# Gate and up of a SwiGLU layer with standing weights and streaming tokens

## Chip, core and metric

The kernel runs on one core of one Trainium2 chip. The metric is the device time of one execution in microseconds (us), smaller is better. A difference of about 0.2% is the least that a measurement of this kernel can tell.

## What is computed

Two layers of a small transformer trunk over 256 tokens of width 1024, all in float32. Each layer has a mixer (a sparse attention whose keys are chosen by an indexer, beside a differential attention) and a SwiGLU feed-forward part of inner width 2816. Cut to what matters here:

```python
for layer in range(DEPTH):                       # 2
    h = rms_norm(x, g_mix[layer])
    ...                                          # projections, two attentions
    x = x + mixed @ w_out[layer]
    h2 = rms_norm(x, g_ffn[layer])
    gate = h2 @ w_gate[layer]                    # 256 x 1024 by 1024 x 2816
    up = h2 @ w_up[layer]
    x = x + (silu(gate) * up) @ w_down[layer]    # 256 x 2816 by 2816 x 1024
return rms_norm(x, g_final)
```

## The kernel before

Tokens lie in two blocks of 128 (`NB = 2`, index b). Every large product is made in a split form: a float32 operand becomes a high part, rounded to the float32r type in which TensorE takes a column a cycle, and a low part, the rest. `mm3` (L205) makes three matmuls of each product: high by high, high by low weight, low by high weight. Activations stand in the array as 128x128 blocks and weights stream, 512 columns at a time.

Weights come in chunks of one megabyte. `load` (L163) issues the DMA on SP's queue into one of three `wraw` buffers; `split_sub` (L181) makes the high part on ScalarE (L186) and the low part on VectorE (L187), in pieces of 1024 columns, into six buffers `whi` and six `wlo`. `ensure` (L197) keeps loads three chunks and splits one chunk ahead in the order of the text.

The order of TensorE's instructions is written by `Weave` (L50): threads yield a delay and events, and `spend` moves a clock on by what each matmul is reckoned to take. ScalarE's and VectorE's instructions are put in order by the scheduler of the framework; each engine runs its queue in order.

The feed-forward part of a layer: `norm` (L360) transposes the residual x of one token block and half, scales it by the gain and splits it, giving `hi_ffn` and `lo_ffn`; the reciprocal of the root mean square, `rstd`, is one number a token and is applied later. Then, for six groups of 512 columns (the last has 256 of gate and 256 of up side by side), `group` (L633) makes gate for both token blocks in two PSUM banks and then up. `after_gate` (L708) applies rstd and silu on ScalarE. `after_up` (L620) multiplies on VectorE, waits DUP = 2.5 us of the Weave's clock, transposes the product in blocks of 128 on TensorE (`pth`), and splits it into `hi_ff` and `lo_ff` for down. Down (L734) lets those stand and streams `w_down`, 22 contraction tiles for two token blocks and two halves; the last six tiles (`TAIL`) are done piece by piece, so that the residual addition (L756) and the final norm (`final`, L762) of one piece run beside the next. In the last layer, the last half of block 1 is cut into two pieces of 256 columns which share one PSUM bank.

PSUM has eight banks (L117), all under one tag.

Of the kernel before, what the change touches and what calls it, by code (L numbers as in the profile page):

```python
# [8 lines left out]
F32 = mybir.dt.float32  # L9
# [8 lines left out]
P = 128  # L18
# [15 lines left out]
DG = 2.0  # L34
DUP = 2.5
DQB = 2.5
# [72 lines left out]
@with_exitstack  # L109
def tile_hybrid_trunk(ctx, tc, x, xT, w_idx, w_in, w_out, w_gate, w_up, w_down, g_final, rope, out):  # L110
    nc = tc.nc
# [11 lines left out]
    NSUB = 1024  # L123
    LASTN = DFF % 512
    chunks = []
# [6 lines left out]
    for L in range(DEPTH):  # L132
        for nm in GROUPS:
            for a, e in ((0, 4), (4, 8)):
                c = add_chunk(w_idx[L, a // 4] if nm == "idx" else w_in[L], range(a, e), COL[nm], NCOL[nm])
                for k in range(a, e):
                    plan[L, nm, k] = c
        for a in (4, 6, 0, 2):
            c = add_chunk(w_out[L], range(a, a + 2), 0, D)
            for k in (a, a + 1):  # L140
                plan[L, "out", k] = c
        for j in range(6):
            if DFF - j * 512 >= 512:
                for nm, w in (("gate", w_gate), ("up", w_up)):
                    for a in range(0, KT, 4):
                        c = add_chunk(w[L], range(a, a + 4), j * 512, 512)
                        for k in range(a, a + 4):
                            plan[L, nm, j, k] = c
            else:

                for a in range(0, KT, 4):
                    c = add_chunk((w_gate[L], w_up[L]), range(a, a + 4), j * 512, 2 * LASTN)
                    for k in range(a, a + 4):
                        plan[L, "both", j, k] = c
# [8 lines left out]
    def load(c):  # L163
        src, kts, c0, n = chunks[c]
        t = pool.tile([P, len(kts), n], F32, tag="wraw", bufs=3, name=f"wraw{c}")
        if n == NCOL["idx"]:
            for k in range(0, len(kts), 2):
                nc.sync.dma_start(t[:, k:k + 2], src[:, k:k + 2])
        elif isinstance(src, tuple):
            for i, w in enumerate(src):  # L170
                nc.sync.dma_start(t[:, :, i * LASTN:(i + 1) * LASTN], w[kts[0] * P:(kts[-1] + 1) * P, c0:c0 + LASTN]
                                  .rearrange("(k p) n -> p k n", p=P))
# [31 lines left out]

    def mm3(outs, act, kt, first, last, second=False):  # L205


        hi, lo = act[kt]
        for ps, whi, wlo in outs:
            nc.tensor.matmul(ps, hi, whi, start=first, stop=False, skip_group_check=second)  # L210
        for ps, whi, wlo in outs:
            nc.tensor.matmul(ps, hi, wlo, start=False, stop=False, skip_group_check=second)  # L212
        for ps, whi, wlo in outs:
            nc.tensor.matmul(ps, lo, whi, start=False, stop=last, skip_group_check=second)  # L214
            W.spend(3 * max(0.107, 0.216 * ps.shape[-1] / 512))
# [87 lines left out]

    def hilo(sc, hi, lo, k0, k1):
        nc.vector.tensor_copy(hi[:, k0:k1], sc[:, k0:k1])
        nc.vector.tensor_tensor(lo[:, k0:k1], sc[:, k0:k1], hi[:, k0:k1].bitcast(F32), op=ALU.subtract)

    def split_psum(pt, name, scales=None, tag="act", bufs=12):

        n = pt.shape[1]  # L310
        tags = tag if isinstance(tag, tuple) else (tag, tag)
        bufs = bufs if isinstance(bufs, list) else [bufs, bufs]
        hi = pool.tile([P, 4, P], F32R, tag=tags[0], bufs=bufs[0], name=f"hi_{name}")
        lo = pool.tile([P, 4, P], F32R, tag=tags[1], bufs=bufs[1], name=f"lo_{name}")
        if scales is None:
# [6 lines left out]
        else:  # L322
            sc = pool.tile([P, 4, P], F32, tag="hff", bufs=3, name=f"sc_{name}")
            for k in range(0, n, 2):
                scaled(sc, pt, scales, k, k + 2)
                hilo(sc, hi, lo, k, k + 2)
        return [(hi[:, k], lo[:, k]) for k in range(n)]

# [13 lines left out]
    acts = {}  # L342
    rstd = {}

    pts = {}
# [7 lines left out]
    def norm_split(kind, L, b, h):  # L353
        key = (kind, L, b)
        acts.setdefault(key, []).extend(
            split_psum(pts.pop(key + (h,)), f"{kind}{L}{b}{h}",
                       scales=[gcol(kind, L, 4 * h + k) for k in range(4)]))
        W.done(("act",) + key + (h,), 2.0)

    def norm(kind, L, b, h):  # L360
# [4 lines left out]
        if h == 1:  # L365
            rstd[kind, L, b] = norm_rstd(b, f"{kind}{L}{b}")


# [250 lines left out]

    def after_up(L, j, b, n, s, ps):  # L620
        hh = pool.tile([P, 512], F32, tag="hff", bufs=3, name=f"hff{L}{j}{b}")
        nc.vector.scalar_tensor_tensor(hh[:, :n], ps[:, :n], rstd["ffn", L, b], s[:, :n], op0=ALU.mult, op1=ALU.mult)
        yield DUP, ()
        pt = bank(f"pth{L}{j}{b}").rearrange("p (k t) -> p k t", k=4)
        for k in range(n // P):
            transpose(pt[:, k], hh[:, k * P:(k + 1) * P])
        t = split_psum(pt[:, :n // P], f"ff{L}{j}{b}", tag=FT[j], bufs=[FTB.get(t, 2) for t in FT[j]])
        for i, e in enumerate(t):
            ffT[L, b, 4 * j + i] = e
        W.done(("ff", L, j, b), 1.8)  # L630

# [36 lines left out]
    def main():  # L668
        for L in range(DEPTH):
# [25 lines left out]
            for b in range(NB):  # L695
                for h in range(2):
# [6 lines left out]
                    W.spawn(norm("ffn", L, b, h))  # L703
            for j in range(6):
                n = min(512, DFF - j * 512)
                silus = {}

                def after_gate(b, ps):  # L708
                    s = pool.tile([P, 512], F32, tag="silu", bufs=2, name=f"silu{L}{j}{b}")
                    nc.scalar.activation(s[:, :n], ps[:, :n], AF.Silu, scale=rstd["ffn", L, b])  # L710
                    silus[b] = s

                if n == 512:
                    yield from group("ffn", L, (L, "gate", j), n, j == 0, after_gate)
                    yield from group("ffn", L, (L, "up", j), n, False,
                                     lambda b, ps: W.spawn(after_up(L, j, b, n, silus[b], ps)))
                else:
                    def after_both(b, ps):
                        after_gate(b, ps)
                        W.spawn(after_up(L, j, b, n, silus[b], ps[:, n:]))  # L720

                    yield from group("ffn", L, (L, "both", j), 2 * n, False, after_both)
            nk = DFF // P
            halves = [(0, 512), (512, 1024)]

            cuts = [list(halves) for b in range(NB)]
            if L + 1 == DEPTH:
                cuts[NB - 1] = [(0, 512), (512, 768), (768, 1024)]
            pd = [[bank(f"dn{L}{b}{h}") for h in range(2)] for b in range(NB)]

            def piece(b, a, e):
                return pd[b][a // 512][:, a % 512:a % 512 + e - a]

            def down(b, cols, kt):  # L734
                w = parts[plan[L, "down", kt], kt]
                mm3([(piece(b, a, e), w[0][:, a:e], w[1][:, a:e]) for a, e in cols], ffT, (L, b, kt),
                    kt == 0, kt == nk - 1, cols[0][0] % 512 > 0)

            TAIL = 6
            for kt in range(nk - TAIL):  # L740
                ensure(plan[L, "down", kt], 3, 2)
                for b in range(NB):
                    yield 0, (("ff", L, kt // 4, b),)
                    down(b, halves, kt)
            ensure(plan[L, "down", nk - 1], 3, 1)
# [3 lines left out]
            for b in range(NB):  # L749
                if L + 1 == DEPTH:  # L750
                    fin = final(b, cuts[b], gfin)
                for h, (a, e) in enumerate(cuts[b]):
                    for kt in range(nk - TAIL, nk):
                        yield 0, (("ff", L, kt // 4, b),)
                        down(b, [(a, e)], kt)
                    nc.vector.tensor_tensor(X[b][:, a:e], piece(b, a, e), X[b][:, a:e], op=ALU.add)  # L756
                    if L + 1 == DEPTH:
                        next(fin)
# [38 lines left out]
    def startup(after):  # L797
        n = NCOL["idx"]
        with tc.manual_schedule(engines={ENG.Activation, ENG.DVE}):
# [18 lines left out]
            def halved(h, b):  # L818
                hi, lo = (pool.tile([P, 4, P], F32R, tag="act", bufs=12, name=f"{w}_mix0{b}{h}") for w in ("hi", "lo"))
                v = sc[h][:, :, b * P:(b + 1) * P]  # L820
# [81 lines left out]
```

## Time and profile before

| | |
|---|---|
| time, median of 3 runs | 638.94 us (638.86 to 638.96) |
| profiled execution, its own time | 638.96 us |
| its span, first to last instruction | 637.1 us |
| TensorE (PE) busy, matmuls | 626.2 us, 98%, 3091 |
| VectorE (DVE) busy | 435.5 us, 68% |
| ScalarE (ACT) busy | 361.2 us, 57% |
| moved from HBM | 108.02 MB |

The span is what the instructions take; some 1.9 us lie around it. Matmuls are pipelined: a 512-column matmul is shown with 0.39 us, but the next starts 0.227 us after it, so a stage is read from starts and not from durations. PEld rows are the loads of the block that stands for the next matmul.

### The profile page before, as it was taken

To read this page: it belongs to the slowest core of one execution; us is meant where nothing else is said; L and a number is where in the kernel's file an instruction comes from. 1 tells how busy PE (TensorE), PEld (TensorE's weight loads), DVE (VectorE), ACT (ScalarE), POOL (GpSimd) and SP (SyncE) were. 2 spreads that over 40 slices of the span, in tenths; PEclk is the share of its full clock that TensorE was granted. 3 is DMA by queue.
4 is the path that set the end of the run, shared out by engine and by line. 5 is a ranking of instruction groups with operands and counts; after the bars stand their busy time and mean duration, and the time that the engine had idled before them with its cause. 6 is when DMAs were issued, how large, how long until landed. Compare 5 with 4: busy or idle time off the path is not lost.

```text
span 637.1 us, 8397 instructions
## 1 busy us (share of the span) xinstructions
PE 626.2 (98%) x3091; PEld 512.0 (80%) x3091; DVE 435.5 (68%) x925; ACT 361.2 (57%) x620; POOL 2.0 (0%) x12
## 2 busy tenths in 40 slices
PE   9999999999999999999999999999999999999995
PEld 5888777888888888888898787878888888888884
DVE  5999997696555456544598999876756555464445
ACT  4877587684454444433477777876744454453331
POOL 1000000000000000000000000000000000000000
PEclk9999999999999999999999999999999999999999
DMA  9854443346665556654286533323755555646511
GB/s 334 288 196 151 139 172 134 133 133 198 199 197 163 192 175 199 198 195 145 67 268 205 188 133 132 133 70 129 246 178 174 196 198 179 196 158 200 193 34 66
DMA packets 49369, 109.61 MB, mean 172 GB/s; under 512 B 1968, under 2 KB 6576, under 8 KB 49328
## 3 DMA queue, kind: packets, MB, share of 16 engines
q1 hardware_dynamic: 48320, 106.96, 50.4%
q10 hardware_dynamic: 1008, 2.12, 0.9%
q8 instruction: 24, 0.39, 0.3%
q14 instruction: 17, 0.14, 0.1%
HBM read 108.02 MB, written 1.05 MB: 171 GB/s over the span
## 4 chain that ended last, share of the span: by engine, by line
PE 81%; DVE 14%; issue 2%; DMA 2%; ACT 1%; ACTq 0%
PE dn L210 6%; PE dn L214 6%; PE dn L212 6%; PE ps_gate L210 6%; PE ps_gate L214 6%; PE ps_gate L212 6%; PE ps_up L214 6%; PE ps_up L212 6%; PE ps_up L210 6%; DVE wlo L187 4%; PE wo L210 2%; PE wo L214 2%; PE wo L212 2%; DVE topk L474 2%; PE pth L218 2%
## 5 line engine op out<-in xcount | busy, mean ns | idle before, releaser
L187 DVE TENSOR_TENSOR wlo<-wraw,whi 128x1024 fp32r<-128x1024 f32 (+1 forms) x200 | 241.3, 1213 | 138.3 <-ACT whi L186 134.3
L186 ACT CAST whi<-wraw 128x1024 fp32r<-128x1024 f32 (+1 forms) x200 | 207.1, 1044 | 147.4 <-PE dn L214 47.5
L210 PE MATMUL ps_gate<-whi,hi_ffn 128*128 128x512 f32 x160 | 64.3, 402 | 0.0
L214 PE MATMUL ps_gate<-whi,lo_ffn 128*128 128x512 f32 x160 | 62.5, 391 | 0.0
L214 PE MATMUL ps_up<-whi,lo_ffn 128*128 128x512 f32 x160 | 62.3, 389 | 0.0
L212 PE MATMUL ps_gate<-wlo,hi_ffn 128*128 128x512 f32 x160 | 62.3, 389 | 0.0
L210 PE MATMUL ps_up<-whi,hi_ffn 128*128 128x512 f32 x160 | 62.2, 389 | 0.0
L212 PE MATMUL ps_up<-wlo,hi_ffn 128*128 128x512 f32 x160 | 62.2, 389 | 0.0
L210 PE MATMUL dn<-whi,hi_ff 128*128 128x512 f32 (+1 forms) x182 | 59.9, 386 | 0.5 <-DVE x L756 0.5
L214 PE MATMUL dn<-whi,lo_ff 128*128 128x512 f32 (+1 forms) x182 | 59.2, 382 | 0.0
L212 PE MATMUL dn<-wlo,hi_ff 128*128 128x512 f32 (+1 forms) x182 | 59.2, 382 | 0.0
L214 PEld LDWEIGHTS dn<-whi,lo_ff 128*128 128x128 f32 x182 | 34.2, 188 | 6.7
L210 PEld LDWEIGHTS dn<-whi,hi_ff 128*128 128x128 f32 x182 | 33.9, 188 | 7.0 <-DVE x L756 0.7
L212 PEld LDWEIGHTS dn<-wlo,hi_ff 128*128 128x128 f32 x182 | 34.2, 188 | 6.6
L214 PEld LDWEIGHTS ps_gate<-whi,lo_ffn 128*128 128x128 f32 x160 | 30.0, 188 | 6.6
L210 PEld LDWEIGHTS ps_up<-whi,hi_ffn 128*128 128x128 f32 x160 | 30.0, 188 | 6.2
L214 PEld LDWEIGHTS ps_up<-whi,lo_ffn 128*128 128x128 f32 x160 | 30.0, 188 | 6.2
L212 PEld LDWEIGHTS ps_up<-wlo,hi_ffn 128*128 128x128 f32 x160 | 30.0, 188 | 6.2
L212 PEld LDWEIGHTS ps_gate<-wlo,hi_ffn 128*128 128x128 f32 x160 | 30.1, 188 | 5.7
L210 PEld LDWEIGHTS ps_gate<-whi,hi_ffn 128*128 128x128 f32 x160 | 30.1, 188 | 5.6
L316 ACT CAST hi_ff<-pth 128x512 fp32r<-128x512 f32 (+1 forms) x24 | 13.1, 548 | 21.1 <-PE pth L218 21.1
L317 DVE TENSOR_TENSOR lo_ff<-pth,hi_ff 128x512 fp32r<-128x512 f32 (+1 forms) x24 | 15.5, 646 | 8.8 <-ACT hi_ff L316 8.8
(346 smaller groups left out, 1081.5 us busy)
## 6 DMA issues: line engine op xcount, KB each, us to landing
wraw<-in_w_in_dram SPq DMA_DIRECT2D x24, 1024.0 KB, 5.1
wraw<-in_w_down_dram SPq DMA_DIRECT2D x22, 1024.0 KB, 5.0
wraw<-in_w_gate_dram SPq DMA_DIRECT2D x20, 1024.0 KB, 5.1
wraw<-in_w_up_dram SPq DMA_DIRECT2D x20, 1024.0 KB, 5.1
wraw<-in_w_out_dram SPq DMA_DIRECT2D x8, 1024.0 KB, 5.0
wraw<-in_w_idx_dram SPq DMA_DIRECT2D x8, 296.0 KB, 3.5
wraw<-in_w_gate_dram SPq DMA_DIRECT2D x4, 512.0 KB, 4.0
wraw<-in_w_up_dram SPq DMA_DIRECT2D x4, 512.0 KB, 5.0
```

Of the source, the lines that this page charges most:

```text
L186: nc.scalar.copy(hi, raw[c][:, s:s + step])
L187: nc.vector.tensor_tensor(lo, raw[c][:, s:s + step], hi.bitcast(F32), op=ALU.subtract)
L210: nc.tensor.matmul(ps, hi, whi, start=first, stop=False, skip_group_check=second)
L212: nc.tensor.matmul(ps, hi, wlo, start=False, stop=False, skip_group_check=second)
L214: nc.tensor.matmul(ps, lo, whi, start=False, stop=last, skip_group_check=second)
L218: nc.tensor.transpose(o, i, ident)
L316: nc.scalar.copy(hi[:, :n], pt)
L317: nc.vector.tensor_tensor(lo[:, :n], pt, hi[:, :n].bitcast(F32), op=ALU.subtract)
L474: nc.vector.match_replace(out=nxt[:, :nk], in_to_replace=m8, in_values=cur[:, :nk], imm_value=TAKEN)
```

## The change

Gate and up are made transposed. A 128x128 block of w_gate or w_up stands, and the tokens stream: the high weights against high and low tokens of both blocks side by side (512 columns), the low weights against the high tokens (256 columns). `ff_mm` makes one unit, a block of 128 inner columns of one matrix, in one PSUM bank; its two halves are added at evacuation (`halves_sum`). The inner dimension then lies on the partitions, as down needs it, and the transposition of the product goes away. rstd now varies along the free dimension: for gate, `norm` transposes rstd, broadcast to 128 columns, into a row of both token blocks (`rows`, DRB = 6.0 us behind the norm); for up, the factor is applied when down's result is added to the residual (`add`). The first two column blocks (BYB = 2) are made one token block at a time. w_gate and w_up are stored on the host as one array `w_ff`, one contiguous megabyte to a block of 128 inner columns. The two last quarter pieces of down get PSUM banks of their own, and what was summed up to then for that half is added to x first.

```diff
+        for i in range(NF):
+
+            plan[L, "ff", i] = add_chunk(w_ff[L, i], range(2), 0, KT * P)
...
+        elif len(src.shape) == 4:
+            nc.sync.dma_start(t, src.rearrange("p m k n -> p m (k n)"))
...
     def norm(kind, L, b, h):
...
         if h == 1:
             rstd[kind, L, b] = norm_rstd(b, f"{kind}{L}{b}")
+            if kind == "ffn":
+                yield DRB, ()
+
+                if b == 0:
+                    rows["ffn", L] = pool.tile([P, S], F32, tag="amask", bufs=2, name=f"rrow{L}")
+                pt = bank(f"ptr{L}{b}")
+                transpose(pt[:, :P], rstd[kind, L, b].to_broadcast([P, P]))
+                nc.scalar.copy(rows["ffn", L][:, b * P:(b + 1) * P], pt[:, :P])
+                if b == NB - 1:
+                    W.done(("rrow", L))
...
-    def after_up(L, j, b, n, s, ps):
-        hh = pool.tile([P, 512], F32, tag="hff", bufs=3, name=f"hff{L}{j}{b}")
-        nc.vector.scalar_tensor_tensor(hh[:, :n], ps[:, :n], rstd["ffn", L, b], s[:, :n], op0=ALU.mult, op1=ALU.mult)
-        yield DUP, ()
-        pt = bank(f"pth{L}{j}{b}").rearrange("p (k t) -> p k t", k=4)
-        for k in range(n // P):
-            transpose(pt[:, k], hh[:, k * P:(k + 1) * P])
-        t = split_psum(pt[:, :n // P], f"ff{L}{j}{b}", tag=FT[j], bufs=[FTB.get(t, 2) for t in FT[j]])
...
+    def ff_mm(L, i, m, ps, bs):
+
+
+        c = plan[L, "ff", i]
+        whi, wlo = parts[c, m]
+        sl = slice(bs[0] * P, (bs[-1] + 1) * P)
+        ps = ps.rearrange("p (t q) -> p t q", t=2)
+        for k in range(KT):
+            yield 0, tuple(("act", "ffn", L, b, k // 4) for b in bs)
+            a = acts["ffn", L, k // 4][k % 4 // 2][:, k % 2]
+            w = slice(k * P, (k + 1) * P)
+            both = lambda: nc.tensor.matmul(ps[:, :, sl], whi[:, w], a[:, :, sl], start=(k == 0), stop=(k == KT - 1))
+            if k == 0:
+                both()
+            nc.tensor.matmul(ps[:, 0, sl], wlo[:, w], a[:, 0, sl], start=False, stop=False)
+            if k > 0:
+                both()
+            W.spend((0.32 + 0.027) if len(bs) == 2 else 0.187)
+
+    def halves_sum(ps, name):
+        t = pool.tile([P, 512], F32, tag="hff", bufs=3, name=name)[:, :S]
+        nc.scalar.copy(t, ps[:, S:])
+        nc.vector.tensor_tensor(t, ps[:, :S], t, op=ALU.add)
+        return t
+
+    silus = {}
+
+    def after_gate(L, i, ps):
+        g = halves_sum(ps, f"gt{L}{i}")
+        nc.vector.tensor_tensor(g, g, rows["ffn", L], op=ALU.mult)
+        s = silus[L, i] = pool.tile([P, 512], F32, tag="silu", bufs=2, name=f"silu{L}{i}")[:, :S]
+        nc.scalar.activation(s, g, AF.Silu)
+
+    def after_up(L, i, ps):
+
+        u = halves_sum(ps, f"up{L}{i}")
+        nc.vector.tensor_tensor(u, u, silus[L, i], op=ALU.mult)
...
+        hi, lo = (t[:, i % 2] for t in fft)
+        nc.scalar.copy(hi, u)
+        nc.vector.tensor_tensor(lo, u, hi.bitcast(F32), op=ALU.subtract)
...
+    def after_ff(L, i, m, ps):
+        yield 0, (("rrow", L),)
+        (after_gate, after_up)[m](L, i, ps)
+
+    def feed_forward(L):
+        units = [(i, m) for i in range(BYB) for m in range(2)]
+        banks = {}
+        for b in range(NB):
+            for i, m in units:
+                ensure(plan[L, "ff", i])
+                if b == 0:
+                    banks[i, m] = bank(f"ff{L}_{i}{m}")
+                yield from ff_mm(L, i, m, banks[i, m], (b,))
+                if b == NB - 1:
+                    W.spawn(after_ff(L, i, m, banks[i, m]))
+        for i in range(BYB, NF):
+            for m in range(2):
+                ensure(plan[L, "ff", i])
+                ps = bank(f"ff{L}_{i}{m}")
+                yield from ff_mm(L, i, m, ps, (0, 1))
+                W.spawn(after_ff(L, i, m, ps))
...
+            def add(b, a, e, ps):
+                nc.vector.scalar_tensor_tensor(X[b][:, a:e], ps[:, :e - a], rstd["ffn", L, b], X[b][:, a:e],
+                                               op0=ALU.mult, op1=ALU.add)
...
+                    if ends and b == NB - 1 and kt == nk - TAIL - 1:
+                        for h in (1, 0):
+                            down(b, halves[h:h + 1], kt, pd[b][h:h + 1], False, h == 1)
+                        add(b, 512, D, pd[b][1])
...
+                if ends and b == NB - 1:
+                    pieces[1:] = [(ae, bank(f"dne{ae[0]}"), True) for ae in ((512, 768), (768, 1024))]
```

## Rows read from the trace of the kernel before

**Rows 1.** The page: busy time by engine; granted clock by 40 slices.
```profile
PE 626.2 (98%) x3091; PEld 512.0 (80%) x3091; DVE 435.5 (68%) x925; ACT 361.2 (57%) x620; POOL 2.0 (0%) x12
...
PEclk9999999999999999999999999999999999999999
```

**Rows 2.** Waits of TensorE: line waited for; us in total, times, longest.
```profile
PE ppt_b L218 <- DVE p_b L530: 2.0, 2, 1.0
...
PE dn L210 <- DVE x L756: 0.5, 1, 0.5
```

**Rows 3.** Timeline, TensorE, both ends of gate and up: start, duration, operation.
```profile
132.94 0.40 PE L212 MATMUL ps_gate<-wlo,hi_ffn 128*128 128x512 f32 x1
...
258.36 0.62 PE L212 MATMUL dn<-wlo,hi_ff 128*128 128x512 f32 x2
```

**Rows 4.** Timeline, TensorE, the last matmuls of down: 512 columns, then 256.
```profile
612.74 0.39 PE L210 MATMUL dn<-whi,hi_ff 128*128 128x512 f32 x1
...
624.75 0.39 PE L214 MATMUL dn<-whi,lo_ff 128*128 128x512 f32 x1
624.98 0.28 PE L210 MATMUL dn<-whi,hi_ff 128*128 128x256 f32 x1
625.09 0.28 PE L212 MATMUL dn<-wlo,hi_ff 128*128 128x256 f32 x1
...
627.01 0.28 PE L214 MATMUL dn<-whi,lo_ff 128*128 128x256 f32 x1
```

**Rows 5.** Timeline, TensorE, eight 128-column matmuls between 512-column ones.
```profile
397.66 0.39 PE L214 MATMUL ps_va<-whi,lo_mix 128*128 128x512 f32 x1
397.89 1.05 PE L445 MATMUL ob<-vb,pT_b 128*128 128x128 f32 x8
...
399.01 0.40 PE L212 MATMUL ps_va<-wlo,hi_mix 128*128 128x512 f32 x1
```

**Rows 6.** Timeline, loads and matmuls of TensorE after the pause in the tail.
```profile
627.80 0.19 PEld L210 LDWEIGHTS dn<-whi,hi_ff 128*128 128x128 f32 x1 [0.72 <-DVE x L756]
...
627.91 0.19 PEld L212 LDWEIGHTS dn<-wlo,hi_ff 128*128 128x128 f32 x1
628.03 0.28 PE L212 MATMUL dn<-wlo,hi_ff 128*128 128x256 f32 x1
```

**Rows 7.** Timeline: last transpositions of the feed-forward norm, last step of its rstd.
```profile
135.49 0.60 PE L218 MATMUL pt_ffn<-ident,x 128*128 128x128 f32 x4
...
141.01 0.16 DVE L296 SCALAR_TENSOR_TENSOR rs_ffn01y<-rs_ffn01t,rs_ffn01y 128x1 f32<-128x1 f32 x1
```

**Rows 8.** Timeline of the tail: VectorE's last additions, TensorE's last matmul.
```profile
628.46 0.69 DVE L773 TENSOR_TENSOR fo<-x,gfin 128x512 f32<-128x512 f32 x1
...
629.94 0.28 PE L214 MATMUL dn<-whi,lo_ff 128*128 128x256 f32 x1
...
630.74 0.41 DVE L756 TENSOR_TENSOR x<-dn,x 128x256 f32<-128x256 f32 x1
```

**Rows 9.** Groups by line and shape, 132 to 258 us: count, busy us, mean ns.
```profile
L187 DVE TENSOR_TENSOR wlo<-wraw,whi 128x1024 fp32r<-128x1024 f32 x47 | 57.4, 1224 | 44.2 <-ACT whi L186 42.3
...
L306 DVE TENSOR_TENSOR lo_ffn<-sc_ffn,hi_ffn 128x256 fp32r<-128x256 f32 x4 | 1.5, 415 | 0.0
...
L186 ACT CAST whi<-wraw 128x1024 fp32r<-128x1024 f32 x46 | 48.3, 1053 | 40.8 <-PE ps_up L214 20.5 <-issue 10.0 <-PE ps_gate L214 8.3
...
L710 ACT ACTIVATE silu<-ps_both,rs_ffn00y 128x256 f32<-128x256 f32 x1 | 0.5, 475 | 1.7 <-PE ps_both L214 1.7
```

**Rows 10.** Windows: busy us of each engine (instructions), clock, DMA share, GB/s.
```profile
0.00:100.00 100.00, 97.48 (x486) 76.44 (x487) 89.26 (x257) 71.38 (x151) 1.96 (x12) 1.00 0.62 214
```

**Rows 11.** Waits of ScalarE: line waited for; us in total, times, longest.
```profile
ACT whi L186 <- PE ps_up L214: 41.0, 32, 3.0
```

**Rows 12.** Timeline, TensorE, 512-column matmuls that follow a run of 296 columns.
```profile
326.43 0.40 PE L210 MATMUL ps_qb<-whi,hi_mix 128*128 128x512 f32 x1
...
327.82 0.39 PE L210 MATMUL ps_qb<-whi,hi_mix 128*128 128x512 f32 x1
```

More of the change, by code (lines that the diff above doesn't have):

```diff
@@ L34 @@
 DG = 2.0
-DUP = 2.5
+BYB = 2
+DRB = 6.0
 DQB = 2.5
@@ L123, in tile_hybrid_trunk @@
     NSUB = 1024
-    LASTN = DFF % 512
+    NF = DFF // P
     chunks = []
@@ L325, in split_psum @@
                 scaled(sc, pt, scales, k, k + 2)
-                hilo(sc, hi, lo, k, k + 2)
-        return [(hi[:, k], lo[:, k]) for k in range(n)]
+                if into is None:
+                    hilo(sc, hi, lo, k, k + 2)
+                else:
+                    hilo(sc, *into[k // 2], k, k + 2, 0)
+        return [] if into is not None else [(hi[:, k], lo[:, k]) for k in range(n)]
     def square_sum(src, acc, name):
@@ L343, in tile_hybrid_trunk @@
     rstd = {}
+    rows = {}
     pts = {}
@@ L354, in norm_split @@
         key = (kind, L, b)
-        acts.setdefault(key, []).extend(
-            split_psum(pts.pop(key + (h,)), f"{kind}{L}{b}{h}",
-                       scales=[gcol(kind, L, 4 * h + k) for k in range(4)]))
+        into = None
+        if kind == "ffn":
+            if b == 0:
+                acts["ffn", L, h] = [pool.tile([P, 2, 2, S], F32R, tag="act", bufs=6, name=f"actT{L}{h}{i}")
+                                     for i in range(2)]
+            into = [[t[:, :, i, b * P:(b + 1) * P] for i in range(2)] for t in acts["ffn", L, h]]
+        r = split_psum(pts.pop(key + (h,)), f"{kind}{L}{b}{h}",
+                       scales=[gcol(kind, L, 4 * h + k) for k in range(4)], into=into)
+        if kind != "ffn":
+            acts.setdefault(key, []).extend(r)
         W.done(("act",) + key + (h,), 2.0)
@@ L703, in main, with down @@
                     W.spawn(norm("ffn", L, b, h))
[L704 to L722, printed above, removed]
+            yield from feed_forward(L)
             nk = DFF // P
             halves = [(0, 512), (512, 1024)]
-            cuts = [list(halves) for b in range(NB)]
-            if L + 1 == DEPTH:
-                cuts[NB - 1] = [(0, 512), (512, 768), (768, 1024)]
             pd = [[bank(f"dn{L}{b}{h}") for h in range(2)] for b in range(NB)]
-            def piece(b, a, e):
-                return pd[b][a // 512][:, a % 512:a % 512 + e - a]
-            def down(b, cols, kt):
+            TAIL = 6
+            def down(b, cols, kt, banks, first, last):
                 w = parts[plan[L, "down", kt], kt]
-                mm3([(piece(b, a, e), w[0][:, a:e], w[1][:, a:e]) for a, e in cols], ffT, (L, b, kt),
-                    kt == 0, kt == nk - 1, cols[0][0] % 512 > 0)
-            TAIL = 6
+                mm3([(ps[:, :e - a], w[0][:, a:e], w[1][:, a:e]) for (a, e), ps in zip(cols, banks)], ffT, (L, b, kt),
+                    first, last)
+            def add(b, a, e, ps):
+                nc.vector.scalar_tensor_tensor(X[b][:, a:e], ps[:, :e - a], rstd["ffn", L, b], X[b][:, a:e],
+                                               op0=ALU.mult, op1=ALU.add)
+            ends = L + 1 == DEPTH
             for kt in range(nk - TAIL):
@@ L749, in main @@
             for b in range(NB):
-                if L + 1 == DEPTH:
-                    fin = final(b, cuts[b], gfin)
-                for h, (a, e) in enumerate(cuts[b]):
+                pieces = [(ae, ps, False) for ae, ps in zip(halves, pd[b])]
+                if ends and b == NB - 1:
+                    pieces[1:] = [(ae, bank(f"dne{ae[0]}"), True) for ae in ((512, 768), (768, 1024))]
+                if ends:
+                    fin = final(b, [p[0] for p in pieces], gfin)
+                for h, ((a, e), ps, own) in enumerate(pieces):
                     for kt in range(nk - TAIL, nk):
[L754 to L757, printed above, removed]
+                        yield 0, (("ff", L, kt),)
+                        down(b, [(a, e)], kt, [ps], own and kt == nk - TAIL, kt == nk - 1)
+                    add(b, a, e, ps)
+                    if ends:
                         next(fin)
```

67 lines of the change are left out of this document (31 added, 36 removed).

## The prediction

> **What bounds the kernel now.** I began with the page: TensorE is busy for 98% of the span at a granted clock of ten tenths in all slices, VectorE for 68% [rows 1]. Then the list of what TensorE waited for: no line waited more than 2.0 us in all, and the only entry of the feed-forward part is 0.5 us before the last piece of the last down projection [rows 2]. None lies in gate and up. So in the feed-forward part the time is the number of matmuls times their pitch (start to start), plus the transpositions between them; other engines count only if they come to stall TensorE. I therefore read the stage boundaries and the pitches of the shapes that the change uses.
>
> Gate and up of layer 0, from their second matmul at 132.94 to the third matmul of down at 258.36, take 125.42 us [rows 3]; layer 1 does the same work and I count it alike. Per layer there are 2 x 5 x 8 x 2 x 3 = 480 matmuls of whole groups and 48 of the last, half-wide group, 528 in all, every one 512 columns wide.
>
> **Pitches.** 512 columns: in the tail, 53 steps from 612.74 to 624.75 give 0.2267 us. 256 columns: 16 steps from 625.09 to 627.01 give 0.120 [rows 4]. The two differ by 0.1067 for 256 columns, which is the 2.4 GHz level, and leave 0.0133 per matmul for each shape. In the stretch of 125.42 us lie 529 steps of 512 columns (119.92 us) and 46 transpositions (42 of the product, 4 of the norm of the second token block): 5.50 us, or 0.120 for a transposition with the slow steps that follow it.
>
> **Removed from TensorE.** Per layer, 528 matmuls (119.69 us) and 44 transpositions of silu(gate)*up: 42 at 0.120 and two more in the down stage at about 0.12, together 5.27 us. Both layers: 239.4 + 10.5 = 249.9 us.
>
> **Added to TensorE.** Now a 128x128 block of weights stands. For both token blocks together, each contraction tile needs one matmul of 512 columns (high weight against high and low tokens) and one of 256 (low weight against high tokens): 0.2267 + 0.120 = 0.3467 us. This is 20 column blocks x 2 matrices x 8 tiles x 2 layers = 640 pairs, 221.9 us. The columns streamed are the same as before; one narrow matmul more per 1536 columns brings its own 0.0133.
>
> The first two column blocks (BYB = 2) are done one token block at a time: 2 x 2 x 2 x 8 x 2 = 128 pairs of 256 and 128 columns. No row shows a 128-column matmul of this type in a row of its like, so I bound it. From below, by the line through the two pitches: 0.120 - 0.0533 = 0.067. From above, 0.112: eight 128-column matmuls with eight weight loads, between the matmul at 397.66 and the second after them at 399.01, take 1.35 - 2 x 0.2267 = 0.90 us [rows 5] (their operands are plain fp32, which may itself take longer). What decides between them is the weight load. After the pause in the tail a load starts at 627.80, the next one at 627.91 and their second matmul at 628.03 [rows 6]: a load takes 0.11 us, and the next starts only when the matmul of the first has started. A narrow stream of 0.053 us can't cover the load of the following weights. I take 0.110, so 0.230 a pair and 29.4 us; the lower bound would give 23.9.
>
> Two transpositions of the broadcast rstd per layer: 4 x 0.15 = 0.6 us, each alone with its slow steps behind it. They wait for rstd: for the second block its last step on VectorE starts at 141.01, the transpositions of that norm at 135.49 [rows 7], so end at about 135.94; the order puts the new one 6.0 us later (DRB), at 142. Cover 0.8 us; without it TensorE would stand for what is missing, once per layer. I put it at nothing.
>
> Sum on TensorE: 221.9 + 29.4 + 0.6 - 249.9 = **+2.0 us**.
>
> **VectorE and ScalarE.** The new evacuation costs per column block on VectorE two sums from PSUM (256 columns: 0.41 [rows 8]) and three operations out of SBUF (0.415 each), beside two weight splits of 1.224 [rows 9]: 2.45 + 0.82 + 1.25 = 4.52 us in 5.55 us of TensorE's time, 81%. ScalarE has two casts of 1.053 and four operations of 256 columns at 0.475 or less [rows 9]: 4.0 us, 72%. Both loads fit, and in the first 100 us VectorE was busy for 89.26 us and TensorE for 97.48 [rows 10]: an engine at 89% need not stall it. The weights are also split well ahead: casts wait for TensorE's release of the old weight buffers, not the other way about [rows 11]. But evacuations now hand over twice between the engines in each pair of units (copy to sum, product to high part), and both queues are in order: what stands behind a waiting sum is the split of coming weights, and TensorE waits for that. Here I take nothing; the price if it fails is a rival below. Extra waits: a unit's PSUM bank is held until both rstd rows are there; eight banks, four units held, up to four for norm and row transpositions, so none is late.
>
> **Loads.** As many bytes, in one contiguous megabyte per column block; a megabyte lands in 5.1 us now, well inside three chunks of lead. Nothing.
>
> **The tail.** The last two quarter pieces get banks of their own, so the matmul held until 627.80 [rows 6] starts without its pause: TensorE is done 0.78 us sooner. But VectorE runs without a break from 628.46 to the last addition at 630.74 [rows 8], while the last matmul had started at 629.94 and runs 0.28: this addition was waiting for VectorE's own queue. I take 0 for the tail; bounds -1.2 (queue reordered so that the add follows its matmul) and +0.2 (the two additions of 0.41 now carry the factor rstd; a quarter more each is an estimate). The other additions of down get the same factor beside other work.
>
> **Sum.** The profiled execution took 638.96 us (span 637.1), as the median 638.94. 638.96 + 2.0 = **640.9**.
>
> **Rivals.**
> *Narrow work is cheaper than I count (faster).* If a 128-column gap follows the stream and not the load, 128 pairs cost 0.043 less: -5.5, 635.4. Likewise, the first 256-column step after a 512 takes 0.11 (624.98 to 625.09 [rows 4]), some 0.007 less by rows of two digits; if every pair had that, 640 x 0.007 = -4.5: 636.4. Against the first stands the load of 0.11 [rows 6]; against the second, that 512 steps after shorter ones are longer by about as much [rows 12]. The Trainium skill ("TensorE: Matmul & The Clock Gate", Back-to-back issue gap) gives a sustained spacing with weight loads of 81 ns for 128 and 131 ns for 512 columns; by its 81 ns I would estimate 640.9 - 128 x 0.029 = 637.2, a case of this rival. The trace differs from the page at 512 columns: 0.2267. Chance of this rival 0.21.
>
> *VectorE and ScalarE become the bound (slower).* Place: the splits of coming weights behind an evacuation that waits for the other engine. It decides when those waits exceed the 1.03 us that VectorE has left per column block. With both queues in the order of the text, the loop silu, cast, two splits, sum, product, high part, low part, sum, product is 0.5 + 1.05 + 2.45 + 0.8 + 0.5 + 0.4 + 0.8 + about 0.3 of handing over = 6.8 us, 1.25 above TensorE's 5.55: over 40 blocks +50 us. The casts' waits [rows 11] speak for splits that run ahead, so a part of it is more plausible: 0.2 a block gives +8: 649. Chance 0.19.
>
> *Mixing widths keeps TensorE in its slow step.* After a run of 296-column matmuls the first six 512-column steps take 0.232 on average (326.43 to 327.82 [rows 12]) before 0.227 returns. If each pair bears one such surplus, 640 x 0.005 = +3.3: 644; two, 647. Chance 0.12.
>
> **How the numbers follow.** The forecast of a TensorE floor that rises by 2 us has 0.48, with its own range 639.3 to 642.3. About 0.2% (1.3 us) is what a measurement of this kernel can tell from no change: 637.7 to 640.2. Faster 0.20 (nearly all of the first rival); same 0.20 (the lower third of the forecast, with a tail that gains); slower 0.60. For eight in ten the range must reach into the first rival and to the nearer ends of the other two: 636.2 to 647.
>
> **What would show it.** Pairs at 0.347 us in the steady part and 0.230 at its start; VectorE about 80% busy there; no wait of TensorE for split weights; no transposition of the product; the stage from first gate matmul to first down matmul about 1 us longer in each layer. Wrong would be: weight loads overlapping a 128-column stream by more than one (then faster), or waits of TensorE for VectorE's low parts (then much slower).

## The result and the profile after

| | before | after |
|---|---|---|
| time, median | 638.95 us (638.86 to 639.01) | 642.25 us (642.00 to 642.76) |
| ratio, 95% interval | | 1.0053 [1.0035, 1.0070] |
| profiled execution, its span | 638.96, 637.1 us | 642.76, 640.9 us |
| forecast | | 640.9 (636.2 to 647) |

The change makes the kernel slower by 3.3 us by the medians, where I had forecast 2.0. Direction and range held; the size did not quite, and the experiments below find the missing part.

The page of the changed kernel, busy time by engine, the granted clock, and the two lines of gate and up (they stand against [rows 1]):

```profile
PE 629.4 (98%) x3487; PEld 529.3 (83%) x3487; DVE 493.5 (77%) x1098; ACT 394.0 (61%) x752; POOL 1.9 (0%) x12
...
PEclk9999999999999999999999999999999999999998
...
L643 PE MATMUL ff<-actT,whi 128*128 128x512 f32 (+1 forms) x768 | 248.8, 385 | 0.0
...
L646 PE MATMUL ff<-actT,wlo 128*128 128x256 f32 (+1 forms) x768 | 192.5, 271 | 0.0
```

TensorE is still the engine that sets the end, at a full clock, and neither line of gate and up has any idle time before it. The list of its waits (line waited for; us in total, times, longest; its three longest entries) agrees:

```profile
PE ppt_b L207 <- DVE p_b L542: 2.1, 2, 1.0
PE warmup L254 <- DVE warm L229: 1.2, 1, 1.2
PE ps_kb L201 <- DVE wlo L176: 0.6, 1, 0.6
```

All of these lie in the mixer or at the start. In the feed-forward part nothing waits for a split weight, an evacuation or a rstd row, and the 0.5 us of down [rows 2] are gone.

Next, where the time lies. Timeline of TensorE in the kernel before, the first transpositions of each layer's feed-forward norm, and in layer 1 the third matmul of down (with [rows 3] for layer 0 and [rows 8] for the end):

```profile
132.27 0.60 PE L218 MATMUL pt_ffn<-ident,x 128*128 128x128 f32 x4
...
443.31 0.60 PE L218 MATMUL pt_ffn<-ident,x 128*128 128x128 f32 x4
...
569.40 0.40 PE L212 MATMUL dn<-wlo,hi_ff 128*128 128x512 f32 x1
```

The same points in the changed kernel, and its last matmul:

```profile
132.81 0.60 PE L207 MATMUL pt_ffn<-ident,x 128*128 128x128 f32 x4
...
261.00 0.61 PE L201 MATMUL dn<-wlo,ffhi 128*128 128x512 f32 x2
...
445.68 0.60 PE L207 MATMUL pt_ffn<-ident,x 128*128 128x128 f32 x4
...
573.88 0.39 PE L201 MATMUL dn<-wlo,ffhi 128*128 128x512 f32 x1
...
633.38 0.28 PE L203 MATMUL dne<-whi,fflo 128*128 128x256 f32 x1
```

| stretch of the profiled executions | before | after | difference |
|---|---|---|---|
| start to the norm of layer 0 | 132.27 | 132.81 | +0.54 |
| gate and up, layer 0 | 126.09 | 128.19 | +2.10 |
| down of layer 0, mixer of layer 1 | 184.95 | 184.68 | -0.27 |
| gate and up, layer 1 | 126.09 | 128.20 | +2.11 |
| down of layer 1 to its last matmul | 60.54 | 59.50 | -1.04 |
| last matmul to the end of the span | 7.16 | 7.52 | +0.36 |
| sum | 637.1 | 640.9 | +3.8 |

The first line isn't the change's: the version e8 below contains the same start and is at 132.33 there. It is probably also why the profiled execution lies 0.5 above its median. Both gate-and-up stages are 2.1 longer. In down, two transpositions a layer are gone; I put the 0.27 of layer 0 down to them, and as much of the 1.04 in layer 1. Of the tail there remains -0.77 for the matmul that no longer waits [rows 6] and +0.36 that is lost again behind it. In terms of the forecast: TensorE's matmuls and transpositions +3.7 instead of +2.0, the tail -0.4 instead of 0.

What the pitches became is read from ends of units. In the timeline two matmuls of L643 stand together (x2) where one unit ends with its wide matmul and the next begins with one, so the distance of two such rows is one unit of eight pairs. First, three units of the narrow start, and then four steady ones:

```profile
137.30 0.46 PE L643 MATMUL ff<-actT,whi 128*128 128x256 f32 x2
...
142.85 0.45 PE L643 MATMUL ff<-actT,whi 128*128 128x256 f32 x2
...
168.04 0.63 PE L643 MATMUL ff<-actT,whi 128*128 128x512 f32 x2
...
170.82 0.62 PE L643 MATMUL ff<-actT,whi 128*128 128x512 f32 x2
...
173.64 0.63 PE L643 MATMUL ff<-actT,whi 128*128 128x512 f32 x2
...
176.41 0.62 PE L643 MATMUL ff<-actT,whi 128*128 128x512 f32 x2
...
179.23 0.63 PE L643 MATMUL ff<-actT,whi 128*128 128x512 f32 x2
```

Three narrow units take 5.55 us: 0.231 a pair, where I took 0.230. Steady units alternate between 2.82 and 2.77 us, 11.19 for four, 0.3497 a pair where I took 0.3467. That is 2.798 a unit instead of 2.773, and for 80 units 1.9 us: the part that the forecast lacked.

### The profile page after: what moved, and what is told of

Its sections match the earlier page's. It is cut to its first block, busy times and chain, and to the rows that moved or that the text cites. A ratio compares the mean times of both kernels' runs of the same rounds, so it can differ in the third digit from the quotient of the medians.

```text
span 640.9 us, 9540 instructions
## 1 busy us (share of the span) xinstructions
PE 629.4 (98%) x3487; PEld 529.3 (83%) x3487; DVE 493.5 (77%) x1098; ACT 394.0 (61%) x752; POOL 1.9 (0%) x12
## 4 chain that ended last, share of the span: by engine, by line
PE 80%; DVE 15%; issue 2%; DMA 2%; ACT 1%; ACTq 0%
PE ff L643 27%; PE ff L646 13%; PE dn L203 6%; PE dn L199 6%; PE dn L201 6%; DVE wlo L176 5%; PE wo L199 2%; PE wo L203 2%; PE wo L201 2%; DVE topk L486 2%; DVE m L484 1%; DVE score L476 1%; PE ps_va L199 1%; PE ps_va L203 1%; PE ps_va L201 1%
## 5 line engine op out<-in xcount | busy, mean ns | idle before, releaser
L643 PE MATMUL ff<-actT,whi 128*128 128x512 f32 (+1 forms) x768 | 248.8, 385 | 0.0
L646 PE MATMUL ff<-actT,wlo 128*128 128x256 f32 (+1 forms) x768 | 192.5, 271 | 0.0
L643 PEld LDWEIGHTS ff<-actT,whi 128*128 128x128 f32 x768 | 137.3, 188 | 21.7
L646 PEld LDWEIGHTS ff<-actT,wlo 128*128 128x128 f32 x768 | 143.9, 189 | 7.1
L199 PE MATMUL dn<-whi,ffhi 128*128 128x512 f32 x170 | 56.2, 391 | 0.0
L203 PE MATMUL dn<-whi,fflo 128*128 128x512 f32 x170 | 56.0, 389 | 0.0
L201 PE MATMUL dn<-wlo,ffhi 128*128 128x512 f32 x170 | 55.9, 389 | 0.0
L203 PEld LDWEIGHTS dn<-whi,fflo 128*128 128x128 f32 x170 | 31.9, 188 | 6.6
L201 PEld LDWEIGHTS dn<-wlo,ffhi 128*128 128x128 f32 x170 | 31.9, 188 | 6.5
L199 PEld LDWEIGHTS dn<-whi,ffhi 128*128 128x128 f32 x170 | 31.9, 188 | 6.5
```

The lines of the kernel that those rows point to most:

```text
L199: nc.tensor.matmul(ps, hi, whi, start=first, stop=False)
L201: nc.tensor.matmul(ps, hi, wlo, start=False, stop=False)
L203: nc.tensor.matmul(ps, lo, whi, start=False, stop=last)
L643: both = lambda: nc.tensor.matmul(ps[:, :, sl], whi[:, w], a[:, :, sl], start=(k == 0), stop=(k == KT - 1))
L646: nc.tensor.matmul(ps[:, 0, sl], wlo[:, w], a[:, 0, sl], start=False, stop=False)
```

## The experiments

Two questions were open: where the surplus of a steady pair comes from (the streams over standing weights, the change of width, the buffers, the other engines), and whether the other terms of the sum are right or hide each other's errors. All times stand against the kernel before, which took 638.98 to 639.04 us when it was measured beside them. Differences of about 1 us and less are at or under the 0.2% that a time can tell; there the starts in the traces carry the reading.

**e1: no narrow start.** All column blocks are made for both token blocks from the beginning.

```diff
-BYB = 2
+BYB = 0
```

> The first two column blocks are also made with both token blocks at once (BYB = 0). If 128 columns are held by the weight load (0.11, 0.23 a pair), 128 narrow pairs (29.4 us) become 64 wide ones (22.4): 7.0 us less work. But nothing is left that needs only token block 0, so TensorE must wait for the norm of block 1 in each layer: by the trace of before it is split at about 139, gate begins at 133.2 and 1.4 us of work on its first half fit between, so some 4.4 us a layer. Net +1.8: about 644. If narrow pairs cost only 0.187 (stream-bound), 24.0 becomes 22.4 and the time is about 649.

Measured: 643.28 us, ratio 1.0066 [1.0051, 1.0081], 1.0 above the changed kernel. The waits of TensorE show what the narrow start is there for (three entries of its list):

```profile
PE ff L643 <- DVE actT L296: 2.6, 2, 1.3
...
PE ptr L207 <- DVE rs_ffn01y L285: 1.6, 1, 1.6
PE ptr L207 <- DVE rs_ffn11y L285: 1.6, 1, 1.6
```

Without it, TensorE stands for the second token block's activations and for its rstd, 5.8 us in all by this list. The list counts a wait from the shown end of the matmul before it, and that end lies behind the point where the next one could have started, so by starts more is lost. Both ends of gate and up in layer 0, as in the table above:

```profile
132.49 0.60 PE L207 MATMUL pt_ffn<-ident,x 128*128 128x128 f32 x4
...
261.18 0.63 PE L201 MATMUL dn<-wlo,ffhi 128*128 128x512 f32 x2
```

These are 128.69 us. The work in them, 44 wide units at 2.797, ten transpositions at 0.11 and two matmuls of down, is 124.6; the same sum for the changed kernel, with 40 wide units and 64 narrow pairs, gives its 128.2 without any pause. TensorE thus stands 4.1 us in each layer, 8.2 in all. What the run saves by pitches is 29.4 for the narrow pairs less 64 x 0.35 = 22.4 for as many wide ones, 7.0. The two leave +1.2, and +1.0 was measured.

**e2: the price of a 128-column step.** In the first two column blocks only the high weights run over the first token block (256 columns, high and low tokens). The low weights wait for the second block and then run once over the high tokens of both (256 columns). No 128-column step is left.

```diff
+            if len(bs) == 1:
+                second = bs[0] > 0
+                nc.tensor.matmul(ps[:, :, sl], whi[:, w], a[:, :, sl], start=(k == 0 and not second), stop=False,
+                                 skip_group_check=True)
...
+                if second:
+                    nc.tensor.matmul(ps[:, 0, :], wlo[:, w], a[:, 0, :], start=False, stop=(k == KT - 1),
+                                     skip_group_check=True)
...
+                continue
```

> Start of the feed-forward part with BYB = 2, but the low-weight matmul waits for token block 1 and then takes both blocks (256 columns): per tile 3 x 0.120 = 0.36 instead of 2 x 0.23 = 0.46, no 128-column stream is left. If the weight load holds narrow streams: 64 x 0.10 = 6.4 us less, less some 1 us a layer of waiting since block 0 alone now fills 3.8 us: about 638. If narrow pairs are stream-bound (0.187, 0.374 for two): 0.9 less and 2 more: about 643.

Measured: 637.88 us, ratio 0.9982 [0.9973, 0.9992], as the price of 0.110 has it, and 1.1 us below the kernel before, about as little as a measurement can tell. Timeline of TensorE at the beginning of this start:

```profile
132.59 2.03 PE L645 MATMUL ff<-actT,whi 128*128 128x256 f32 x15
```

Its waits there:

```profile
PE ff L645 <- DVE actT L296: 1.0, 2, 0.5
...
PE ptr L207 <- DVE rs_ffn01y L285: 0.2, 1, 0.2
PE ptr L207 <- DVE rs_ffn11y L285: 0.2, 1, 0.2
```

Fifteen 256-column matmuls, the last one's own 0.28 taken off, are 14 steps in 1.75 us, 0.125 with the slow first one behind the transpositions. A 128-column step takes 0.110 (a pair's 0.231 less 0.120) for half the columns; two of them in place of one step of 256 are 0.10 lost, 64 times, 6.4 us. The run gives back 4.4: its start is shorter, and the waits above come up in it, 1.4 us by the list. By starts they are longer; the matmuls before and behind them in layer 0:

```profile
137.88 0.28 PE L649 MATMUL ff<-actT,wlo 128*128 128x256 f32 x1
138.65 0.38 PE L645 MATMUL ff<-actT,whi 128*128 128x256 f32 x1 [0.48 <-DVE actT L296]
...
141.74 0.28 PE L649 MATMUL ff<-actT,wlo 128*128 128x256 f32 x1
142.21 0.32 PE L207 MATMUL ptr<-ident,rs_ffn01y 128*128 128x128 f32 x1 [0.19 <-DVE rs_ffn01y L285]
```

They are steps of 0.77 and 0.47 where 0.12 is regular, 1.0 us lost in each layer, and 6.4 less 2.0 is the 4.4. So rstd, which I had called covered, is so only while the narrow start is long. The Trainium skill ("TensorE: Matmul & The Clock Gate", Back-to-back issue gap) has 81 ns for a matmul of 128 columns with its weight load; the trace doesn't agree here, with 0.110 (e3 below has such matmuls in a row).

**e3: one change of width per unit.** All eight 512-column matmuls of a unit, then all eight of 256.

```diff
-            both = lambda: nc.tensor.matmul(ps[:, :, sl], whi[:, w], a[:, :, sl], start=(k == 0), stop=(k == KT - 1))
-            if k == 0:
-                both()
-            nc.tensor.matmul(ps[:, 0, sl], wlo[:, w], a[:, 0, sl], start=False, stop=False)
-            if k > 0:
-                both()
...
+            nc.tensor.matmul(ps[:, :, sl], whi[:, w], a[:, :, sl], start=(k == 0), stop=False)
...
+        for k in range(KT):
...
+            nc.tensor.matmul(ps[:, 0, sl], wlo[:, w], a[:, 0, sl], start=False, stop=(k == KT - 1))
...
```

> In each unit first all eight high-weight matmuls (512 columns), then all eight low-weight ones (256). Same work. If changing widths costs something (wide pairs measured 0.3496 against 0.3467 of the two pitches), the units come down to 2.77 us and the time by up to 2: 640. If the excess belongs to something else (other engines, buffers, the synchronisation at a unit's start), 642.2 within 0.5.

Measured: 641.93 us, ratio 1.0044 [1.0028, 1.0061]. A gain of 0.3, less than the times can tell apart and not the 2 that the theory gives, so the surplus isn't one of equal size for each change of width. Timeline of TensorE, starts of three units in a row:

```profile
162.15 2.00 PE L643 MATMUL ff<-actT,whi 128*128 128x512 f32 x8
163.99 1.11 PE L648 MATMUL ff<-actT,wlo 128*128 128x256 f32 x8
164.94 0.40 PE L643 MATMUL ff<-actT,whi 128*128 128x512 f32 x1
...
167.73 0.63 PE L643 MATMUL ff<-actT,whi 128*128 128x512 f32 x2
```

Every unit now takes 2.79 us, 0.02 above 2.773, and the alternation is gone. The eight wide matmuls take 1.84 us (162.15 to 163.99), 0.03 more than 8 x 0.2267, and the eight narrow ones 0.95, 0.01 less than 8 x 0.120. The start-to-start times in the trace put the surplus where [rows 12] have it: the first five wide steps of a unit take 0.235, 0.236, 0.228, 0.232 and 0.231, the others 0.227. The first narrow step takes 0.113 and the others 0.120. One change to narrow work and back thus costs 0.02 in this order. In the changed kernel, by the same count, a wide step takes 0.234, 0.007 more than in a run of its like, and a narrow one 0.116, 0.004 less; eight pairs cost 0.024. That leaves two readings, once per return or a little per narrow step; e9 tells them apart.

The run's narrow start also has what no row before showed, eight 128-column matmuls in a row:

```profile
137.92 1.01 PE L648 MATMUL ff<-actT,wlo 128*128 128x128 f32 x8
138.76 1.17 PE L643 MATMUL ff<-actT,whi 128*128 128x256 f32 x8
```

They take 0.84 us. Start to start, seven of the steps are 0.11 each; the first, behind a 256-column one, is 0.06, and the first 256-column step behind them pays that back with 0.17. The weight loads beside them start 0.11 apart too. That fits my reason, the load, but no run changes the load alone.

**e4: gate and up exchange their weight buffers.** w_up lies in the first half of each loaded megabyte.

```diff
-        whi, wlo = parts[c, m]
+        whi, wlo = parts[c, 1 - m]
...
-        "w_ff": np.stack([w_gate, w_up]).reshape(2, DEPTH, KT, P, DFF // P, P).transpose(1, 4, 3, 0, 2, 5),
+        "w_ff": np.stack([w_up, w_gate]).reshape(2, DEPTH, KT, P, DFF // P, P).transpose(1, 4, 3, 0, 2, 5),
```

> The two matrices swap places in the weight array, so gate uses the second weight buffer of a chunk and up the first; the order on TensorE and everything else stays. Time 642.2 within 0.5 by every theory. In the trace after, each unit of gate takes 2.817 us and each unit of up 2.777. If this goes with the weight buffer, up becomes the slow one; if with what other engines do beside it or with the accumulation bank, gate stays slow.

Measured: 642.27 us, ratio 1.0051 [1.0036, 1.0066]; the units still alternate. In layer 0 the long unit is now that of up, in layer 1 it is still that of gate, so neither the buffer nor the work beside gate or up makes a unit long. Why long and short ones alternate is open. It carries no time: the mean of a long and a short unit is 2.797 in every run with this order.

**e5: no narrow step in the steady part.** The low weights run over high and low tokens, 512 columns.

```diff
-            nc.tensor.matmul(ps[:, 0, sl], wlo[:, w], a[:, 0, sl], start=False, stop=False)
+            nc.tensor.matmul(ps[:, :, sl], wlo[:, w], a[:, :, sl], start=False, stop=False)
...
```

> The low-weight matmul runs over high and low tokens, so every steady pair is two 512-column matmuls and no narrow one (one product more is computed than the reference needs; the additional columns are known work). Theory: a 512-column step with standing weights has the pace of before, 0.2267 us, and the surplus of the changed kernel (0.350 instead of 0.3467 a pair) comes from the 256-column neighbours. Then 640 pairs cost 0.4533 - 0.350 = 0.1033 more each, +66.1 us, and 128 narrow pairs 0.010 more each (two 256-column steps of 0.120 instead of 0.230), +1.3: 709.7 us, with all 512 steps at 0.227 in the trace. Rival: streams over standing weights are slower by themselves, 0.234 each as the mean 512 step of the changed kernel's trace: 640 x (0.468 - 0.350) = +75.5, +1.3: 719.1 us.

Measured: 709.75 us, ratio 1.1107 [1.1090, 1.1124], against 709.7 and 719.1. Timeline of TensorE, the end of the narrow start and of the first wide unit, and two later ends of units, three units apart:

```profile
148.59 0.52 PE L643 MATMUL ff<-actT,whi 128*128 128x256 f32 x2
...
152.14 0.62 PE L643 MATMUL ff<-actT,whi 128*128 128x512 f32 x2
...
166.64 0.62 PE L643 MATMUL ff<-actT,whi 128*128 128x512 f32 x2
...
177.52 0.62 PE L643 MATMUL ff<-actT,whi 128*128 128x512 f32 x2
```

Three units from 166.64 to 177.52 are 48 steps of 0.2267: over standing weights a 512-column step has the very pace of before [rows 4]. So the 0.234 that it has in the changed kernel comes from its narrow neighbours. The first wide unit shows one return by itself: from the last narrow matmul at 148.59 to the last wide one of the unit at 152.14 are 3.55 us, where 0.12 and 15 x 0.2267 would be 3.52. That is the 0.03 of e3's wide steps again, here with no narrow step behind it that gives 0.01 back.

**e6: what the other engines need.** The low-weight matmuls are left out.

```diff
-            nc.tensor.matmul(ps[:, 0, sl], wlo[:, w], a[:, 0, sl], start=False, stop=False)
...
```

> The low-weight matmuls of gate and up are left out (their product is missing from the result), all other work stays. TensorE then needs 16 x 0.2267 = 3.63 us for a column block, VectorE 4.5 by its durations, so the period of a block shows what VectorE and ScalarE need with all their waits for each other. If the handing over costs little, 4.5 to 4.7 us a block instead of 5.59: 40 blocks x 0.9 to 1.05, 600 to 606 us. If the in-order queues add waits that TensorE's 5.59 us only just covers, 5.2 us or more a block: 627 us or more.

Measured, in a single execution: 568.24 us. Both expectations are far too high. Busy times in a window of 50 us (PE, PEld, DVE, ACT, POOL; then clock, DMA share, GB/s):

```profile
150.00:200.00 50.00, 50.00 (x223) 41.39 (x222) 48.85 (x91) 40.78 (x80) 0.00 (x0) 1.00 0.68 244
```

VectorE's timeline in it:

```profile
160.30 1.22 DVE L176 TENSOR_TENSOR wlo<-wraw,whi 128x1024 fp32r<-128x1024 f32 x1
161.44 0.42 DVE L675 TENSOR_TENSOR fflo<-up,ffhi 128x256 fp32r<-128x256 f32 x1
161.77 0.42 DVE L653 TENSOR_TENSOR up<-ff,up 128x256 f32<-128x256 f32 x1
...
163.11 1.22 DVE L176 TENSOR_TENSOR wlo<-wraw,whi 128x1024 fp32r<-128x1024 f32 x1
```

My price of VectorE was made of durations, and durations overlap here: an operation of 0.42 lets the next one start after 0.333 (161.44 to 163.11 are five of them), one of 1.22 after 1.14. Seven instructions a block are then 2 x 1.14 + 5 x 0.333 = 3.95 us and not 4.52, and 91 instructions in 50 us are 13 blocks of 3.85. TensorE isn't held in this window: 223 steps of 0.2267 fill it. It gets ahead of VectorE and waits for it afterwards, in down (one entry of its list):

```profile
PE dn L201 <- DVE wlo L176: 7.4, 2, 3.8
```

So the run's 74.0 us below the changed kernel don't give VectorE's period; the window does. VectorE, which waits for ScalarE twice in each pair of units, is still nearly without a pause at 3.9 us a block. The in-order loop of 6.8 us, the rival that I had priced at 50 us, doesn't exist: the queues run ahead of each other.

**e7: the price of what was removed.** The kernel before makes each of the 88 transpositions of the product twice.

```diff
-        for k in range(n // P):
+        for k in list(range(n // P)) * 2:
```

> The kernel before with each of the 88 transpositions of silu(gate)*up done twice (same result), which measures the price of the removed term by itself. At 0.120 us each with the slow steps behind it: +10.5, 649.5 us. If the slow steps come once for a group and a further transposition costs only its stream: 0.107 or less each, 648.4 us or less. If they lay beside other work, 639 us.

Measured: 648.29 us, ratio 1.0145 [1.0131, 1.0159]: +9.3 us, 0.106 for one more transposition in a group. The 0.120 of the forecast is thus about 0.106 for the transposition itself, and the rest slow wide steps behind its group, which a longer group doesn't raise. Where all of them go, both parts go, so the 10.5 stands. It is the first sign that slow steps come once per group.

**e8: a longer start without 128-column steps.** e2 with three column blocks split by token block and the rstd row one microsecond later.

```diff
-BYB = 2
-DRB = 6.0
+BYB = 3
+DRB = 7.0
```

> The version with the low-weight matmul put off to the second token block, now with three column blocks split by token block instead of two, and the rstd transposition 7 us after the norm instead of 6. Theory: the two pauses of 0.5 us for the second block's activations and the two of 0.2 us for rstd go (-1.4), four more units of 2.88 instead of 2.80 us cost 0.3: 636.8 us. Rival: six PSUM banks held leave two for norm and rstd transpositions, which then wait: 637.9 to 640 us.

Measured: 636.03 us, ratio 0.9954 [0.9942, 0.9967]. It is below the expectation, and TensorE has no wait left in the feed-forward part. The expectation took e2's waits from the list, as 1.4 us; with the 2.0 that they cost by starts it would have been 636.2. Its start, for the first line of the table above:

```profile
132.33 0.60 PE L207 MATMUL pt_ffn<-ident,x 128*128 128x128 f32 x4
```

**e9: one return to wide work per block.** Gate's and up's sixteen 512-column matmuls, then sixteen of 256.

```diff
...
+            pss = [bank(f"ff{L}_{i}{m}") for m in range(2)]
+            for low in (False, True):
+                for m, ps in enumerate(pss):
+                    yield from ff_run(L, i, m, ps, low)
+                    if low:
+                        W.spawn(after_ff(L, i, m, ps))
```

> Gate and up of a column block together: sixteen 512-column matmuls, then sixteen of 256, so that TensorE comes back from narrow to wide work once per block instead of once per unit. In the run with one return per unit a unit took 2.793 us instead of 8 x 0.3467 = 2.773. Theory: the surplus comes once per group of narrow steps, up to some 0.027 a group (first wide unit after the narrow start of the run with wide low matmuls). Then 40 groups x 0.020 to 0.027 replace 80 x 0.024 of the changed kernel: 642.25 - 0.8 to -1.1 = 641.2 to 641.4 us, a block at 5.567 to 5.574. Rival: each narrow step leaves its own 0.0025 behind, however grouped: a block at 5.586 us, 641.9 us as in that run.

Measured: 641.14 us, ratio 1.0033 [1.0021, 1.0045], 1.1 below the changed kernel and 0.8 below e3. Timeline of TensorE, starts of three blocks:

```profile
164.88 3.82 PE L662 MATMUL ff<-actT,whi 128*128 128x512 f32 x16
168.54 2.08 PE L659 MATMUL ff<-actT,wlo 128*128 128x256 f32 x16
170.45 3.82 PE L662 MATMUL ff<-actT,whi 128*128 128x512 f32 x16
...
176.02 2.23 PE L662 MATMUL ff<-actT,whi 128*128 128x512 f32 x9
```

A block takes 5.57 us, 0.02 above 16 x 0.3467 = 5.547, with twice as many narrow steps in its group as in e3 and the same surplus. Its sixteen wide matmuls take 3.66 us, 0.03 more than 16 x 0.2267, its narrow ones 1.91, 0.01 less than 16 x 0.120, as in e3. Once per group it is, not per narrow step; the totals, 0.8 us apart, agree but could hardly tell it.

**e10: both together.** e8 with the order of e9 in its 38 remaining blocks.

```diff
         for i in range(BYB, NF):
...
+            for low in (False, True):
+                for m, ps in enumerate(pss):
+                    yield from ff_run(L, i, m, ps, low)
```

> Three column blocks split by token block with the low-weight matmul put off to the second (636.03 us by its run), and in the other 38 blocks the grouping of gate and up. If the surplus comes once per group: 38 x (5.594 - 5.57) = -0.9, 635.1 us. If each narrow step leaves its own: 38 x 0.008 = -0.3, 635.7 us. If gate's evacuation, which now comes only one run of narrow steps ahead of up's, makes TensorE wait for VectorE: above 636.1 us.

Measured: 634.89 us, ratio 0.9935 [0.9921, 0.9948]: 4.1 us below the kernel before and 7.4 below the changed one, with no wait of TensorE in the feed-forward part; the longest one left is that of all runs in the mixer:

```profile
PE ppt_b L207 <- DVE p_b L542: 2.0, 2, 1.0
...
```

## Why the prediction held, step by step

- **What bounds it: right.** TensorE by count times pitch, before and after; no wait in gate and up.
- **Removed, 249.9 us: right.** 512 columns at 0.2267 come back over standing weights (e5), and the transpositions with their slow steps are consistent with e7.
- **Wide pairs, 221.9 us: too low, and this is the step that failed.** I added two pitches that had been read in runs of one shape. Alternating, a pair takes 0.3497: 223.8 us, +1.9. I had seen both halves of it and set them against each other as about equal: the shorter narrow step behind a wide one and the longer wide steps behind narrow ones. They aren't equal. Of the 0.007 that a wide step takes longer, a narrow one gives 0.004 back. The rival on mixed widths had named the mechanism, from [rows 12], with 0.005 a pair and a chance of 0.12. Its sign was right and its price too high. After a longer group of narrow steps, a return to wide work costs 0.03 once, of which the next first narrow step gives 0.01 back (e3, e9, the first wide unit of e5); where a narrow step follows each wide one, a pair bears only 0.003. With this term the forecast would have been 642.8; the tail's 0.4 taken off, 642.4.
- **Narrow pairs, 29.4 us: right.** 0.231 measured; e2 gives the 128-column step its price, with its waits counted by starts, and e3 shows it in a row of its like. That the weight load sets it is likely and not shown. The lower bound of 0.067, and with it the rival of cheaper narrow work, is out.
- **rstd, 0.6 us: right,** with its cover. Its two transpositions a layer wait for nothing. e1 shows the price without cover, 1.6 us in each layer by the list of waits, and e2 0.2, or 0.35 by starts.
- **VectorE and ScalarE at nothing: right, for a price that was too high.** Durations gave 81% and the window of after shows as much busy time. By starts it is 3.9 us of 5.59, 70% (e6). The rival that they become the bound was further off than its chance of 0.19 said.
- **The tail at 0: nearly.** The matmul starts without its pause, as foreseen, and the last addition waits for VectorE's queue, as foreseen. VectorE's timeline at the end of the changed kernel:

```profile
633.20 0.69 DVE L835 TENSOR_TENSOR fo<-x,gfin 128x512 f32<-128x512 f32 x1
...
634.48 0.21 DVE L837 TENSOR_SCALAR pre_fin<-ss_fin,pre_fin 128x1 f32<-128x1 f32 x1
634.61 0.48 DVE L789 SCALAR_TENSOR_TENSOR x<-dne,rs_ffn11y,x 128x256 f32<-128x256 f32 x1
```

  The addition starts 1.23 us after the start of the last matmul at 633.38, in the kernel before 0.80 after it [rows 8]. Of the 0.77 that TensorE gains, 0.36 is lost again behind it and 0.4 remains, within my bounds of -1.2 and +0.2. No run changed the tail alone.

## What to carry to other kernels

Pitches read in runs of one shape needn't add up in a mixed order; here their sum was 0.9% too low. Price the order, or group the shapes, which here was worth 1.1 us of 642. Before narrow steps are put in to cover a start, see what pitch they have: 128 columns took nearly as long here as 256. Putting the partner matmul off until its columns are there, with a third column block to keep the cover, turned a loss of 3.3 us into a gain of 3.0 (e8). And an engine's load and its waits are better read from starts than from durations: by durations VectorE looked some 15% fuller than it was, and e1 and e2 seemed not to add up.

## What the hardware showed that I had not expected

- The surplus on wide steps after narrow ones is paid once per group and hardly depends on its length: 0.03 us over five wide steps, after 8 narrow steps (e3), 16 (e9) or the long narrow start (e5), all at a full granted clock. The first narrow step of a group gives 0.01 of it back. Where it comes from no run shows.
- Units of one and the same work alternate strictly between 2.82 and 2.77 us when widths alternate, and which matrix has the long one can differ from layer to layer (e4). Open.
- VectorE starts an operation 0.08 to 0.09 us before the one ahead of it is shown to end, so that five of 0.42 take 1.67 us (e6).
